# A paused generator is stopped only at the end of a weight tile

## The chip, the core and the metric

One NeuronCore of a Trainium2 chip runs the whole program. The metric is the device time of one execution in microseconds; shown is the median of several runs. TensorE (PE) multiplies matrices into PSUM, VectorE (DVE), ScalarE (ACT) and GpSimd (POOL) work element by element, SyncE (SP) issues the DMAs. The engines run side by side and wait for each other through semaphores; each works through its own instructions in a fixed order.

## The reference

The reference is a two-layer trunk for 1024 tokens of width 1024, in float32: a layer of RWKV-7 time mixing with an MLP, then a layer of forgetting attention with an MLP. What bears on the change is the dense work around the two mixers:

```python
y = y * ln_w.astype(jnp.float32) + ln_b.astype(jnp.float32)
...
y = (y + bonus.reshape(bsz, T, D_MODEL)).astype(h.dtype)
return (y * g) @ wo, v_first
...
x = x + (1.0 + gt1) * y
h = modulate(rms_norm(x, norm_mlp_g[i]), sh2, sc2)
x = x + (1.0 + gt2) * sq_relu_mlp(h, mlp_up[i], mlp_down[i])
...
def sq_relu_mlp(h, w_up, w_down):
    return jnp.square(jax.nn.relu(h @ w_up)) @ w_down
```

The width of the MLP is 4096. In `wo`, `w_up` and `w_down` lie most of the matrix products.

## The kernel before

Activations stand transposed, width on the 128 partitions, and the 1024 tokens are two halves of 512 columns. A float32 product is made of three products of a shorter float type: an operand `a` is split into a rounded part and the rest (`hh`, `hl` for activations of the projections, `mh`, `ml` inside the MLP, `wh`, `wl` for weights), and `mm3` (lines 120 to 128) issues rounded by rounded (L124), rounded weight by rest (L126) and rest of the weight by rounded (L128).

A weight tile is 128 x 1024 floats. `load_w` (L107) brings it into `wraw` by a DMA on SP's queue, casts it to `wh` on ACT (L116) and takes the difference `wl` on POOL (L117). Each of the three names has two buffers (`NW = (2, 2)`), shared by all streams of weights of the program. A buffer can be taken for a new tile when the last reader of the old tile is done. For one half of the tokens a weight tile serves 24 products of 512 columns.

`proj` (L150) multiplies one set of activations by a list of weight tiles; the first `lead` of them are loaded together. It is a generator that yields after each `mm3`, so that one stream of dense work can be advanced step by step beside something else. `mlp` is one too: sixteen chunks, each with two up tiles (`up`, through `proj`, 16 steps for one half) and two down tiles of the chunk before (`down`, 16 steps). A down tile holds four output blocks of two steps each; after the two steps DVE adds the block to the residual stream `x` (L1016). `take(g, n)` advances a generator by `n` steps, `drain` to its end, `beside` advances one at a given pace while another runs.

The first half's dense work of layer 0, called `m0`, runs beside the recurrent scan, which leaves PE time. When the scan ends, `run` (L347 ff.) goes on in this program order: activations of the second half are loaded and split (`gated(1, hp1)`), `m0` is taken `ND[0]` = 20 steps further, the second half's output projection (`wo`, eight tiles, `lead=2`) is run to its end, two steps of the second half's MLP `m1` make its norm (squares on ACT, L222; sums on POOL, L226; a product with a matrix of ones on PE, L228), `m0` is taken 40 steps and drained, and `m1` follows, beside the vectors of the next layer. In the last stage `phase_out` does the same with another `m0` of layer 1: it runs beside the second half's attention, is then taken `NF` = 36 steps, and the second half's output projection of attention follows.

The program order is only the first word: a scheduler that models the engines' time (`schedule_with_timeline_sim`) puts the instructions of each engine into their final order, and the buffers follow from the program order. In the names of the order, a number after a tile's name is the allocation, `pj`, `pk` are PSUM banks of products, `x06` is block 6 of the first half's residual stream, `x10` block 0 of the second half's; in attention `ps` are scores, `P0`, `P1` softmax tiles (exponentials on ACT, L1296), `pt` their transposes, `po` the sums of values.

Of the kernel before, what the change touches and what calls it, by code (L numbers as in the profile page):

```python
# [26 lines left out]
KT = 8  # L27
# [48 lines left out]
class K:  # L76
# [69 lines left out]
    def take(self, g, n):  # L146
        for _ in range(n):
            next(g, None)

    def proj(self, hs, src, mts, evac, lead=1):  # L150

        mts = list(mts)
        for g in [mts[:lead]] + [[m] for m in mts[lead:]]:
            w = [self.load_w(src(m)) for m in g]
            ps = [[self.bank() for _ in hs] for _ in g]
            for js in ([[j] for j in range(len(hs))] if len(g) > 1 else [range(len(hs))]):
                for k in range(KT):
                    for i in range(len(g)):
                        self.mm3([ps[i][j] for j in js], w[i][0][:, k], w[i][1][:, k], [hs[j] for j in js], k, k == 0, k == KT - 1)
                        yield  # L160
            for i, m in enumerate(g):
                for p, h in zip(ps[i], hs):
                    evac(m, h[0], p)
# [84 lines left out]
    def run(self, stop=99):  # L248
        tc, nc, ap = self.tc, self.nc, self.ap
        V, S = nc.vector, nc.scalar  # L250
        with ExitStack() as es:
# [49 lines left out]
            self.wp = self.pool(es, "wring", 3)  # L301
            self.weng = nc.gpsimd
            self.after_w = False
            pg = self.pool(es, "pg", space=PSUM)
            self.banks, self.nbank = [(pg, "pj", 2)], 0
            self.smalls, self.nsmall = [(pg, "pms", 1)], 0
# [15 lines left out]
            def beside():  # L322
                yield from dense
                el.close()
                self.xq = self.pool(e1, "x0", side="right")
                self.hp = self.pool(ed, "hp", 8, side="right")
                self.mid = self.pool(eg, "mid", 3, side="right")
                while self.ngated < KT:
                    yield
                x[0] = self.load_x(self.xq, 0)  # L330
                hs = self.gated(0, self.hp)
                yield from self.proj([hs], wo, range(KT), self.residual(x, self.G[:, 0:8]), lead=2)
                yield from self.mlp(x, 0, (0,), self.hp, self.mid)
            m0 = beside()
# [14 lines left out]
            with ExitStack() as e2:  # L349
                self.mod_pool = self.pool(e2, "mp"), 2, D  # L350
                hs = self.gated(1, hp1)
                self.take(m0, self.ND[0])
                self.drain(self.proj([hs], wo, range(KT), self.residual(x, self.G[:, 0:8]), lead=2))
                m1 = self.mlp(x, 0, (1,), hp1, md)
                self.take(m1, 2)
                self.take(m0, self.ND[1])
                self.drain(m0)
                self.take(m1, 40)

                def mods():  # L360
                    for j in range(6):
                        yield from self.layer_mod(1, j)
                    for j in range(2):
                        yield from self.mod(ap["kvmodw"], j * D, PC["kvmodb"] + j * 8, self.md[:, 96 + j * 8:104 + j * 8])
                self.after_w = True
                self.beside(mods(), m1, self.NMD)
                for o, j in ((16, 2), (24, 5)):
                    V.tensor_scalar(out=self.G[:, o:o + 8], in0=self.mdc(1, j), scalar1=1.0, scalar2=None, op0=ALU.add)
                self.gains(self.col("nmix1", 0, 8), self.mdc(1, 1), self.A[:, 16:24])
                self.gains(self.col("nmlp1", 0, 8), self.mdc(1, 4), self.A[:, 24:32])  # L370
                self.gains(self.col("kvg", 0, 8), self.md[:, 104:112], self.A[:, 32:40])
                self.take(m1, 100)
                rs = self.rs = [xq.tile([128, HT], F32, name=f"rs{j}") for j in range(2)]
                self.rms(x[0], rs[0])
                kv = self.norm_half(x, 0, rs[0], self.A[:, 32:40], self.md[:, 96:104], hp)
                q0 = self.norm_half(x, 0, rs[0], self.A[:, 16:24], self.mdc(1, 0), hp2)
                self.drain(m1)
# [652 lines left out]
    def mlp(self, x, l, js, hp, md):  # L1030

        nc, ap = self.nc, self.ap
        hs = []
        for j in js:
            rs = md.tile([128, HT], F32, name="mr", tag="mr", bufs=2)
            yield from self.rms_g(x[j], rs)
            hs.append(self.norm_half(x, j, rs, self.A[:, 8 + 16 * l:16 + 16 * l], self.mdc(l, 3), hp))
        gain = self.G[:, 8 + 16 * l:16 + 16 * l]
        mid = {}

        def up(c):
            def evac(m, j, ps):
                h = mid[m, j] = md.tile([128, HT], F32R, name="mh", tag="mh"), md.tile([128, HT], F32R, name="ml", tag="ml")
                r = md.tile([128, HT], F32, name="mr", tag="mr", bufs=2)
                nc.scalar.activation(out=r, in_=ps, func=AF.Relu)
                nc.vector.tensor_tensor(out=r, in0=ps, in1=r, op=ALU.mult)  # L1046
                self.split(*h, r)
            yield from self.proj(hs, lambda m: ap["up"][l][m], range(c * 2, c * 2 + 2), evac, lead=2 if c == 0 else 1)

        def down(c):  # L1050
            ms = [[(j, [mid[c * 2 + k, j][0] for k in range(2)], [mid[c * 2 + k, j][1] for k in range(2)]) for j in js]][0]
            evac = self.residual(x, gain)
            for q in range(2):
                wh, wl = self.load_w(ap["down"][l][c * 2 + q], (128, 2, 4, 128))
                for i in range(4):
                    ps = [self.bank() for _ in js]
                    for k in range(2):
                        self.mm3(ps, wh[:, k, i], wl[:, k, i], ms, k, k == 0, k == 1)
                        yield
                    for j, p in zip(js, ps):  # L1060
                        evac(q * 4 + i, j, p)

        yield from up(0)
        for c in range(1, 16):
            yield from up(c)
            yield from down(c - 1)
        yield from down(15)


# [138 lines left out]
    def phase_out(self, x, hp, pg, es):  # L1208
        with ExitStack() as em:
            md = self.pool(em, "mid1", 3, side="right")  # L1210

            def first():
                yield from self.out_fox(x, 0, hp)
                yield from self.mlp(x, 1, (0,), hp, md)
            m0 = first()
            with ExitStack() as ea:
                wp = self.pool(ea, "att1", 2)
                psa = self.pool(ea, "psa1", 1, space=PSUM)
                self.beside(self.attend(1, wp, psa), m0, self.NM)
            px = self.pool(es, "px2", space=PSUM)  # L1220
            self.banks = [(pg, "pj", 2)] * 2 + [(px, "pk", 4)] * 4
            self.smalls = [(pg, "pms", 1), (px, "pmt", 1)]
            hp1 = self.pool(es, "hp1", 8)
            md1 = self.pool(es, "mid2", 6)
            self.take(m0, self.NF)
            self.drain(self.out_fox(x, 1, hp1))
            m1 = self.mlp(x, 1, (1,), hp1, md1)
            self.take(m1, 2)
            self.drain(m0)
        self.take(m1, 100)  # L1230
        fin = self.pool(es, "fin", 8)
        self.beside(self.phase_final(x, 0, fin), m1, 4)
        self.drain(m1)
        self.drain(self.phase_final(x, 1, fin))
# [235 lines left out]
```

## Time and profile before

| | us |
|---|---|
| median of 3 runs (3393.43 to 3404.93) | 3394.25 |
| profiled execution | 3394.05 |
| its span, first to last instruction | 3392.1 |
| PE busy | 3214.4 |
| DVE busy | 1943.0 |
| ACT busy | 1432.8 |
| POOL busy | 1358.7 |

The profile shows one execution. Busy times of the engines overlap, so they don't add up to the span. A row of the view of stretches gives the busy time of each engine between two moments (counted from the start of the span) and the mean clock that TensorE was granted, as a share of full speed. A row of the view in time order gives the start of an instruction, its duration, its line and tiles, and in brackets how long its engine had been idle before it and which instruction released it. Products on PE are pipelined: their durations overlap, and the distance of two starts tells the pace.

### The profile page before, as it was taken

The page shows a single profiled execution, that of the slowest core. Times are in us where ns is not written, and L with a number is a line of the kernel's source. Part 1 is how long each engine was busy: PE and PEld are TensorE (multiplying, and loading weights), DVE is VectorE, ACT ScalarE, POOL GpSimd, SP SyncE. Part 2 cuts the span into 40 slices and gives each one's busy share as a digit, 9 for nine tenths or more (in the row PEclk, how much of TensorE's full clock was granted, in tenths as well). Part 3 has the DMA queues.
Part 4 walks back from the last instruction along what each step waited for, and adds up shares of the span by engine and source line. Part 5 has one row for each costly group of instructions (what it writes and reads, how often), then busy time and mean ns, then how long its engine had stood idle before and what let it go on. Part 6 is the DMA issues. An engine that isn't in the chain of part 4 may idle for free.

```text
span 3392.1 us, 50350 instructions
## 1 busy us (share of the span) xinstructions
PE 3214.4 (95%) x19108; PEld 2438.4 (72%) x19108; DVE 1943.0 (57%) x3239; ACT 1432.8 (42%) x2284; POOL 1358.7 (40%) x868
## 2 busy tenths in 40 slices
PE   4898999999999999899999999999999999999997
PEld 2456666666777776678887777777778888778886
DVE  7496765766556534167786433555566666454344
ACT  3642236523433223242233556667555544332323
POOL 3364432333333233354444432444423333454444
PEclk7899999899999999899999999999999999999999
DMA  7374344355333223236752233666544443232222
GB/s 276 98 234 151 95 128 135 116 152 150 88 102 102 85 76 125 68 111 224 229 187 88 85 131 119 207 203 182 177 128 136 144 134 100 88 111 95 98 98 83
DMA packets 294065, 452.90 MB, mean 134 GB/s; under 512 B 114720, under 2 KB 170432, under 8 KB 293824
## 3 DMA queue, kind: packets, MB, share of 16 engines
q1 hardware_dynamic: 293824, 449.68, 42.3%
q8 instruction: 152, 2.49, 0.3%
q14 instruction: 89, 0.73, 0.1%
HBM read 371.25 MB, written 78.32 MB: 133 GB/s over the span
## 4 chain that ended last, share of the span: by engine, by line
PE 50%; DVE 4%; ACT 2%; DMA 1%; issue 1%; POOL 1%; SPq 0%; DVEq 0%; ACTq 0%; POOLq 0%
PE pj L124 8%; PE pj L128 7%; PE pj L126 7%; PE pk L128 7%; PE pk L124 7%; PE pk L126 7%; PE pt L1328 2%; PE po L1313 1%; PE po L1314 1%; PE ps L1285 1%; PE ps L1286 1%; DVE t L239 1%; DVE hl L241 1%; DVE x L1016 1%; DVE modacc L185 0%
## 5 line engine op out<-in xcount | busy, mean ns | idle before, releaser
L117 POOL TENSOR_TENSOR wl<-wraw,wh 128x1024 fp32r<-128x1024 f32 x385 | 947.7, 2462 | 1231.7 <-ACT wh L116 1162.6
L116 ACT CAST wh<-wraw 128x1024 fp32r<-128x1024 f32 x385 | 402.6, 1046 | 822.0 <-PE pk L126 359.2
L124 PE MATMUL pj<-hh,wh 128*128 128x512 f32 x1120 | 448.6, 408 | 7.4 <-DVE sq L1090 2.7
L128 PE MATMUL pj<-hh,wl 128*128 128x512 f32 x1120 | 445.1, 403 | 5.5 <-POOL wl L117 5.5
L126 PE MATMUL pj<-hl,wh 128*128 128x512 f32 x1120 | 443.2, 401 | 0.0
L1016 DVE SCALAR_TENSOR_TENSOR x<-pj,G,x 128x512 f32<-128x512 f32 x304 | 225.8, 747 | 164.3 <-PE pj L128 162.2
L128 PE MATMUL pk<-hh,wl 128*128 128x512 f32 x688 | 272.1, 402 | 8.6 <-POOL wl L117 8.6
L124 PE MATMUL pk<-hh,wh 128*128 128x512 f32 x688 | 270.2, 398 | 8.9 <-ACT wh L116 7.8
L126 PE MATMUL pk<-hl,wh 128*128 128x512 f32 x688 | 267.3, 395 | 0.0
L124 PEld LDWEIGHTS pj<-hh,wh 128*128 128x128 f32 x1120 | 210.9, 189 | 61.9 <-issue 4.5
L1016 DVE SCALAR_TENSOR_TENSOR x<-pk,G,x 128x512 f32<-128x512 f32 x240 | 176.2, 746 | 135.7 <-PE pk L128 135.2
L128 PEld LDWEIGHTS pj<-hh,wl 128*128 128x128 f32 x1120 | 210.6, 188 | 58.9 <-POOL wl L117 7.7
L126 PEld LDWEIGHTS pj<-hl,wh 128*128 128x128 f32 x1120 | 211.1, 189 | 48.1 <-issue 2.4
L124 PE MATMUL pj<-mh,wh 128*128 128x512 f32 x564 | 236.9, 421 | 6.0 <-DVE mr L1046 3.0
L126 PE MATMUL pj<-ml,wh 128*128 128x512 f32 x564 | 224.3, 398 | 0.0
L128 PE MATMUL pj<-mh,wl 128*128 128x512 f32 x564 | 219.4, 399 | 2.4 <-POOL wl L117 2.4
L124 PE MATMUL pk<-mh,wh 128*128 128x512 f32 x460 | 182.1, 398 | 8.9 <-DVE mr L1046 5.4
L166 ACT CAST mh<-mr 128x512 fp32r<-128x512 f32 x128 | 79.5, 621 | 250.6 <-PE pj L128 109.1
L126 PE MATMUL pk<-ml,wh 128*128 128x512 f32 x460 | 181.7, 395 | 0.0
L185 DVE SCALAR_TENSOR_TENSOR modacc<-modw,cact,modacc 128x1024 f32<-128x1024 f32 x98 | 155.1, 1583 | 31.0 <-DMA modw<-in_modw_dram 22.5
L128 PE MATMUL pk<-mh,wl 128*128 128x512 f32 x460 | 166.6, 397 | 0.0
L124 PEld LDWEIGHTS pk<-hh,wh 128*128 128x128 f32 x688 | 130.7, 190 | 42.8 <-ACT wh L116 11.6
(334 smaller groups left out, 6493.2 us busy)
## 6 DMA issues: line engine op xcount, KB each, us to landing
wraw<-in_up_dram SPq DMA_DIRECT2D x128, 512.0 KB
wraw<-in_down_dram SPq DMA_DIRECT2D x128, 512.0 KB
modw<-in_modw_dram SPq DMA_DIRECT2D x96, 512.0 KB
wraw<-in_wqg_dram SPq DMA_DIRECT2D x32, 512.0 KB
wraw<-in_wk_dram SPq DMA_DIRECT2D x24, 512.0 KB
wraw<-in_wv_dram SPq DMA_DIRECT2D x24, 512.0 KB
x<-in_xT_dram SPq DMA_DIRECT2D x32, 256.0 KB
wraw<-in_wr_dram SPq DMA_DIRECT2D x16, 512.0 KB
```

The costliest lines, as they stand in the source:

```text
L116: nc.scalar.copy(out=wh, in_=raw)
L117: self.weng.tensor_tensor(out=wl, in0=raw, in1=wh.bitcast(F32), op=ALU.subtract)
L124: mm(out=p, lhsT=wh, rhs=hh[k], start=first, stop=False)
L126: mm(out=p, lhsT=wh, rhs=hl[k], start=False, stop=False)
L128: mm(out=p, lhsT=wl, rhs=hh[k], start=False, stop=last)
L166: self.nc.scalar.copy(out=out_h, in_=src)
L185: nc.vector.scalar_tensor_tensor(out=acc, in0=w, scalar=ck, in1=acc, op0=ALU.mult, op1=ALU.add)
L239: nc.vector.scalar_tensor_tensor(out=t, in0=x[k], scalar=A[:, k:k + 1], in1=rs, op0=ALU.mult, op1=ALU.mult)
L241: nc.vector.scalar_tensor_tensor(out=hl[k], in0=t, scalar=sh[:, k:k + 1], in1=hh[k].bitcast(F32), op0=ALU.add, op1=ALU.subtract)
L1016: self.nc.vector.scalar_tensor_tensor(out=x[j][m], in0=ps, scalar=gain[:, m:m + 1], in1=x[j][m], op0=ALU.mult, op1=ALU.add)
L1285: PE.matmul(out=o[:, 0:r], lhsT=qs[:, q], rhs=kh[:, i * n:i * n + r], start=True, stop=False)
L1328: PE.transpose(out=pt[:, i * 256 + b * 128:i * 256 + (b + 1) * 128], in_=Ps[b][:, (k + i) * 128:(k + i + 1) * 128], identity=ident)
```

## The change

A flag `partial` is kept: true after a step if some weight tile that the stream has loaded has products still to come, false after the last product of all loaded tiles. A new function `take_tiles` takes the given number of steps and then goes on until the flag is false. It replaces `take` at the two places where the first half's stream is stopped before the second half's projection.

```diff
+    def take_tiles(self, g, n):
+
+        self.take(g, n)
+        while self.partial:
+            next(g, None)
...
                 for k in range(KT):
                     for i in range(len(g)):
                         self.mm3([ps[i][j] for j in js], w[i][0][:, k], w[i][1][:, k], [hs[j] for j in js], k, k == 0, k == KT - 1)
+                        self.partial = not (js[-1] == len(hs) - 1 and k == KT - 1 and i == len(g) - 1)
                         yield
...
             self.after_w = False
+            self.partial = False
...
                 hs = self.gated(1, hp1)
-                self.take(m0, self.ND[0])
+                self.take_tiles(m0, self.ND[0])
                 self.drain(self.proj([hs], wo, range(KT), self.residual(x, self.G[:, 0:8]), lead=2))
...
                     for k in range(2):
                         self.mm3(ps, wh[:, k, i], wl[:, k, i], ms, k, k == 0, k == 1)
+                        self.partial = i < 3 or k == 0
                         yield
...
             md1 = self.pool(es, "mid2", 6)
-            self.take(m0, self.NF)
+            self.take_tiles(m0, self.NF)
             self.drain(self.out_fox(x, 1, hp1))
```

At the first place 20 steps end in the middle of a down tile, behind its second block of four; the loop goes on for four steps. At the second place 36 steps end where the flag is false, and nothing is added. All later lines of the file have numbers that are higher by 6 to 9.

On DVE, at the end of the scan, the residual updates show the order in which blocks are finished. Before (L1016 is the update):

```order
L1016 SCALAR_TENSOR_TENSOR x04_7389<-pj_12541,G_88,x04_7389 128x512
L1016 SCALAR_TENSOR_TENSOR x05_7390<-pj_12549,G_88,x05_7390 128x512
L1016 SCALAR_TENSOR_TENSOR x10_12379<-pk_12568,G_88,x10_12379 128x512
L1016 SCALAR_TENSOR_TENSOR x11_12380<-pk_12569,G_88,x11_12380 128x512
L1016 SCALAR_TENSOR_TENSOR x12_12381<-pk_12626,G_88,x12_12381 128x512
L1016 SCALAR_TENSOR_TENSOR x13_12382<-pk_12658,G_88,x13_12382 128x512
L1016 SCALAR_TENSOR_TENSOR x14_12383<-pj_12690,G_88,x14_12383 128x512
L1016 SCALAR_TENSOR_TENSOR x15_12384<-pj_12722,G_88,x15_12384 128x512
L1016 SCALAR_TENSOR_TENSOR x16_12385<-pk_12754,G_88,x16_12385 128x512
L1016 SCALAR_TENSOR_TENSOR x06_7391<-pk_12839,G_88,x06_7391 128x512
L1016 SCALAR_TENSOR_TENSOR x07_7392<-pk_12847,G_88,x07_7392 128x512
```

And DVE at the same place in the changed kernel (L1024 is the update now):

```order
L1024 SCALAR_TENSOR_TENSOR x04_7389<-pj_12541,G_88,x04_7389 128x512
L1024 SCALAR_TENSOR_TENSOR x05_7390<-pj_12549,G_88,x05_7390 128x512
L1024 SCALAR_TENSOR_TENSOR x06_7391<-pk_12557,G_88,x06_7391 128x512
L1024 SCALAR_TENSOR_TENSOR x07_7392<-pk_12565,G_88,x07_7392 128x512
L174 TENSOR_TENSOR ml_12491<-mr_12492,mh_12490 128x512
L1024 SCALAR_TENSOR_TENSOR x10_12379<-pk_12584,G_88,x10_12379 128x512
L1024 SCALAR_TENSOR_TENSOR x11_12380<-pk_12585,G_88,x11_12380 128x512
L1024 SCALAR_TENSOR_TENSOR x12_12381<-pj_12642,G_88,x12_12381 128x512
```

Blocks 6 and 7 of the first half, the last two of the down tile, moved from behind the seventh projection tile to ahead of the first; PE's products stand in the same order, and from PE's row 4056 of 13010 the two orders are alike up to row 8700.

On ACT, at the same place, before (L116 casts a weight tile, L222 squares a block of the second half):

```order
L116 CAST wh_12557<-wraw_12556 128x1024
L116 CAST wh_12563<-wraw_12562 128x1024
L222 ACTIVATE t_12814<-x10_12379 128x512
L116 CAST wh_12621<-wraw_12620 128x1024
L222 ACTIVATE t_12816<-x11_12380 128x512
```

And on ACT in the changed kernel (L173 is the split's cast, L229 the square):

```order
L116 CAST wh_12573<-wraw_12572 128x1024
L173 CAST mh_12490<-mr_12492 128x512
L116 CAST wh_12579<-wraw_12578 128x1024
L116 CAST wh_12637<-wraw_12636 128x1024
L229 ACTIVATE t_12830<-x10_12379 128x512
```

The split of m0's last up block, `mh_12490`, stood behind the last projection cast and now stands behind the first; its buffer comes free with the last products of the down tile.

On PE between rows 8700 and 9221, in the second half's attention beside the first MLP tiles of layer 1's `m0`, the scheduler orders some pieces differently. Before (L1285, L1286, L1288 are scores, L1328 transposes):

```order
L124 MATMUL pj_21832<-hh_21778,wh_21821 128x512
L124 MATMUL pj_21833<-hh_21778,wh_21827 128x512
L126 MATMUL pj_21832<-hl_21786,wh_21821 128x512
L128 MATMUL pj_21832<-hh_21778,wl_21822 128x512
L126 MATMUL pj_21833<-hl_21786,wh_21827 128x512
L128 MATMUL pj_21833<-hh_21778,wl_21828 128x512
L124 MATMUL pj_21832<-hh_21779,wh_21821 128x512
L124 MATMUL pj_21833<-hh_21779,wh_21827 128x512
L1285 MATMUL ps_22018<-kh_21488,qs_21489 128x448
L1286 MATMUL ps_22018<-ka_21490,qa_21491 128x448
```

And on PE in the changed kernel (L1294, L1295 and L1297 are the scores, L1337 the transposes):

```order
L124 MATMUL pj_21832<-hh_21778,wh_21821 128x512
L124 MATMUL pj_21833<-hh_21778,wh_21827 128x512
L1294 MATMUL ps_22018<-kh_21488,qs_21489 128x448
L1295 MATMUL ps_22018<-ka_21490,qa_21491 128x448
L1337 MATMUL pt_22041<-cs_60,P1_21927 128x128
L1337 MATMUL pt_22041<-cs_60,P0_21882 128x128
```

The scores of the next block stood behind the last step but one of the tile pair and now stand ahead of it. From row 9221 on the two orders are alike again.

## Rows read from the trace of the kernel before

**Rows 1.** The page: span, and PE's busy time, share and instruction count.

```profile
span 3392.1 us, 50350 instructions
...
PE 3214.4 (95%) x19108; PEld 2438.4 (72%) x19108; DVE 1943.0 (57%) x3239; ACT 1432.8 (42%) x2284; POOL 1358.7 (40%) x868
```

**Rows 2.** Stretches: start:end, length, busy us (count) by engine, PE clock, DMA share, GB/s.

```profile
1336.00:1414.00 78.00, 61.87 (x211) 45.17 (x211) 8.96 (x14) 13.13 (x17) 26.64 (x14) 0.87 0.17 55
1346.00:1356.00 10.00, 7.65 (x24) 5.49 (x24) 0.75 (x1) 1.61 (x2) 2.12 (x1) 0.83 0.15 53
1414.00:1464.00 50.00, 50.00 (x215) 39.89 (x214) 18.85 (x25) 13.93 (x18) 23.41 (x10) 1.00 0.29 93
```

**Rows 3.** PE's waits, 1336 to 1414: waiter <- releaser: total us, times, longest.

```profile
PE pk L128 <- POOL wl L117: 7.0, 5, 1.7
PE pk L124 <- ACT wh L116: 4.8, 5, 1.0
PE pj L128 <- POOL wl L117: 3.4, 2, 1.7
PE pj L124 <- ACT wh L116: 0.9, 1, 0.9
```

**Rows 4.** PE in time order: start, us, instruction, idle before [us <- releaser].

```profile
1336.52 0.40 PE L124 MATMUL pk<-hh,wh 128*128 128x512 f32 x1
...
1337.65 0.39 PE L124 MATMUL pk<-hh,wh 128*128 128x512 f32 x1
...
1342.21 0.39 PE L128 MATMUL pk<-hh,wl 128*128 128x512 f32 x1
1343.55 0.50 PE L124 MATMUL pk<-hh,wh 128*128 128x512 f32 x1 [0.95 <-ACT wh L116]
...
1345.98 0.50 PE L128 MATMUL pk<-hh,wl 128*128 128x512 f32 x1 [1.70 <-POOL wl L117]
...
1383.60 1.02 PE L228 MATMUL pmt<-t,ones_d 128*128 128x512 f32 x2
...
1405.27 0.50 PE L124 MATMUL pk<-hh,wh 128*128 128x512 f32 x1 [0.95 <-ACT wh L116]
...
1405.84 0.40 PE L124 MATMUL pk<-mh,wh 128*128 128x512 f32 x1
...
1408.64 0.39 PE L128 MATMUL pk<-hh,wl 128*128 128x512 f32 x1
...
1413.65 0.40 PE L124 MATMUL pj<-hh,wh 128*128 128x512 f32 x1
```

**Rows 5.** ACT and POOL in time order around the projection.

```profile
1333.73 1.05 ACT L116 CAST wh<-wraw 128x1024 fp32r<-128x1024 f32 x1 [2.34 <-PE pk L126]
1342.45 1.04 ACT L116 CAST wh<-wraw 128x1024 fp32r<-128x1024 f32 x1 [7.67 <-PE pk L126]
...
1408.14 0.62 ACT L166 CAST mh<-mr 128x512 fp32r<-128x512 f32 x1 [2.36 <-PE pk L128]
...
1334.85 2.40 POOL L117 TENSOR_TENSOR wl<-wraw,wh 128x1024 fp32r<-128x1024 f32 x1 [1.99 <-ACT wh L116]
```

**Rows 6.** Two weight loads, from issue on SP to the cast that waited.

```profile
412.63 0.40 SPq L115 DMA_DIRECT2D wraw<-in_wr_dram  x1
418.10 1.05 ACT L116 CAST wh<-wraw 128x1024 fp32r<-128x1024 f32 x1 [0.77 <-DMA wraw<-in_wr_dram]
...
538.62 0.42 SPq L115 DMA_DIRECT2D wraw<-in_wk_dram  x1
542.66 1.05 ACT L116 CAST wh<-wraw 128x1024 fp32r<-128x1024 f32 x1 [1.69 <-DMA wraw<-in_wk_dram]
```

**Rows 7.** Two stretches of the second half's attention, and one wait of PE.

```profile
2440.00:2471.00 31.00, 26.26 (x148) 21.05 (x146) 20.12 (x38) 19.31 (x39) 13.37 (x11) 0.93 0.48 140
2471.00:2600.00 129.00, 128.32 (x678) 106.46 (x679) 83.95 (x156) 68.19 (x146) 42.54 (x31) 0.98 0.44 130
...
2464.86 0.42 PE L1285 MATMUL ps<-kh,qs 128*128 128x320 f32 x1 [2.23 <-ACT P L1296]
```

## The prediction

> **What bounds the kernel now.** The page comes first: TensorE (PE) is busy for 3214.4 of 3392.1 us, so about 178 us of the span are PE idle time, and any time won has to come from there or from the clock [rows 1]. The profiled execution took 3394.05 us, 1.95 us more than its span and 0.2 us below the median of the three runs, so the sum is made against 3394.05 and read against the median unchanged.
>
> The view by stretches comes next, for the place that the diff names: the second half's output projection. Between 1336 and 1414 us PE is busy for only 61.87 of 78 us and its mean granted clock is 0.87; right behind it, in 1414 to 1464, the first half's MLP runs 50.00 of 50 us at clock 1.00, with weight tiles of the same size and again 24 products for each [rows 2]. So the hole belongs to the stage, not to this kind of work. The list of PE's waits says who makes it: 7.0 + 4.8 + 3.4 + 0.9 = 16.1 us, all for the two steps that split a weight tile, the cast `wh` on ACT and the difference `wl` on POOL [rows 3].
>
> In time order a pattern repeats. The first projection tile runs freely: 20 products start within 1342.21 - 1337.65 = 4.56 us, 0.228 us each. Then PE waits 0.95 us for `wh`, issues two products, waits 1.70 us for `wl`, and so on for every tile; the second tile starts at 1343.55 and the eighth at 1405.27, six periods of (1405.27 - 1343.55) / 6 = 10.29 us where 24 x 0.228 = 5.47 us is the work [rows 4]. ACT shows why: the cast at 1342.45 stood idle for 7.67 us and was let go by PE's L126, the last reader of the `wh` of the tile just finished [rows 5]. With two free buffers it would wait for the tile before that one. One of the two is missing: it holds the down tile of m0, whose last 12 products come only at 1405.84 to 1408.64, inside the eighth projection tile [rows 4].
>
> Of the 10.29 us, 5.47 is work and 2.65 is the two waits. The other 2.17 comes with the clock: in 1346 to 1356 the grant is 0.83, which between the levels of 1.2 and 2.4 GHz means that 3.4 of 10 us ran at half, 1.7 us of them lost [rows 2]; the remaining 0.5 is the slower start after a wait.
>
> **The change part by part.** The second call, in the last stage, adds nothing: 36 steps end there where m0's flag is already false, so no step is moved. The first call moves four steps of m0 ahead of the projection: 12 products and two residual updates on VectorE (DVE). Their weights are loaded and split, their operands exist, and no DMA is moved with them (the 8 projection loads keep their place on SP's queue).
>
> The stretch from the first projection product (1336.52) to the first product of m0's next tile (1413.65) takes 77.1 us now [rows 4]. Afterwards it holds:
> the 12 moved products, 1408.64 - 1405.84 = 2.8 us;
> 192 projection products at 0.228 us, 43.8 us;
> one norm sum (L228), now hidden in a wait, at its shown 1.02 us.
> That is 47.6 us, a gain of 29.5 us. With the pace of the next stretch, 50 us for 215 records or 0.2326 each [rows 2], the 192 cost 44.7 us and the gain is 28.6. I take 0.228, because it was measured on the same operands.
>
> What must hide behind PE for this? Each tile needs a cast (1.05 us) and a difference (2.40 us), about 3.5 us [rows 5], and with both buffers it has one whole tile time, 5.47 us, for that. A raw tile's slot is free again when its difference is done; two loads that were really waited for took 542.66 - 538.62 = 4.0 and 418.10 - 412.63 = 5.5 us from issue to the cast [rows 6]. Load, cast and difference make 7.5 to 9.0 us in the 10.9 us of two tiles. The norm's squares (ACT) and sums (POOL) lie in the rest.
>
> The tightest place is the second tile. On ACT the split of `mh`, which waited until 1408.14 for the held products, now stands between the first and the second projection cast. It can go when the 12 products end, at about 1336.5 + 2.8 = 1339.3; 0.62 for it, 1.05 and 2.40 for cast and difference, and the tile is ready near 1343.5, while PE asks for it at 1339.3 + 5.5 = 1344.8. The cover is 1.3 us. If it failed, one pattern of 4.8 us (10.29 - 5.47) would be back. The first tile's cast and difference stay at 1333.73 and 1334.85 [rows 5] and are now covered by the moved products. For small waits left over I put 0.5 us, between 0 and 4.8, near the low end because the next stretch with the same two buffers shows none.
>
> From row 4056 of PE to row 8700 the order is what it was, so everything until about 2471 us should only come earlier. From there to row 9221 the scheduler orders attention of the second half and m0's first MLP tiles differently: scores come before instead of after the last steps of a tile pair. That stretch, 2471 to 2600, is 128.32 of 129 us busy [rows 7], so at most 0.7 us can be won. Loss is bounded by the 31 us before it, where one chain of waits (2.23 us for a softmax tile the longest) cost 31 - 26.26 = 4.7 us of idle time and a mean clock of 0.93, another 2.2 us [rows 7]; about 7 us for such a break. I take 0, by the stretch's own row.
>
> Sum: 3394.05 - 29.5 + 0.5 = 3365 us.
>
> **Rivals.**
> A, the helpers become the bound. Two buffers free, but loads or splits late, so that a tile takes longer than 5.47 us. It decides when a load needs over 10.9 - 3.5 = 7.4 us. A load of 9 us would make a tile (9 + 3.5) / 2 = 6.25 us, eight of them 6 us more: 3371 us. Against it: the loads of 4.0 and 5.5 us, and the next stretch without a wait.
>
> B, only the pauses come back. If the half clock had another cause than the pauses, the gain would be the 16.1 us of rows 3: 3378 us. For it: no single pause is longer than 1.70 us, yet the clock falls in every period. Against it: the clock is 1.00 in the stretch behind, with the same work and no pause. The Trainium skill, TensorE: Matmul & The Clock Gate, section What's actually happening, puts half clock down to an idle engine and full clock to a busy one; taken strictly, these short pauses with products between them leave the engine busy, the fall would be something else, and 3378 us would follow. The trace speaks against that reading, as said.
>
> C, the change doesn't do what it says: the missing buffer is held by something else and the pattern stays. The time would be 3394 us. Against it: the cast's releaser is the tile just finished, and the pattern ends with the held products.
>
> D, slower: breaks like the one before 2471 us in the reordered attention. About 40 places in the order of PE differ there; at 7 us for each break four would eat the gain, and beyond 0.5% slower it needs (29 + 17) / 7 = 7 of them: 3411 us and more. For it: the transposes of a softmax tile now come sooner behind its scores, with a weight cast and a ReLU ahead of the exponentials on ACT. Against it: those chains lie between long products, as in the 128.32 of 129 us now.
>
> **How the numbers follow.** Forecast 0.86, A 0.05, B 0.03, C 0.04, D 0.02. The forecast's own range goes from 3394.05 - 29.5 - 0.7 = 3364 to 3365 + 7 = 3372; the low end gets some 4 us more for the spread between executions, the high end 3 us for A and a second small wait: 3360 to 3375. About 0.5%, 17 us, is what a measurement of this kernel can tell from no change. Faster by more than that, below 3377: forecast and A, 0.91. Within it: B and C, 0.07. Slower: D, 0.02.
>
> **What would show it.** Right: in the stretch of the second half's projection some 48 us instead of 77, PE busy throughout at clock 1.00, no wait for `wh` or `wl`, and casts let go by the tile before the last; everything up to the attention of the second half 29 us earlier, and the loss of clock near 2450 unchanged. Wrong: PE waits on the raw loads or on `wl` of the second tile (A), a clock below 1 without pauses (B), the old period of 10.3 us (C), or new PE waits for softmax tiles behind about 2440 us (D). The forecast fails as a whole if the projection was already hidden behind something that ends later; but PE is the only engine that works on there, and what follows waits for its products.

## The result, and the profile after

| | before | after |
|---|---|---|
| median of the runs | 3396.16 us (4 runs, 3393.43 to 3404.93) | 3369.24 us (4 runs, 3365.42 to 3374.15) |
| profiled execution | 3394.05 us, span 3392.1 | 3365.42 us, span 3363.6 |
| stage of the second half's projection | 77.13 us | 47.26 us |

The medians differ by 26.9 us. The ratio that is estimated from the single executions is 0.9915, with a 95% interval of 0.9899 to 0.9931, which is 28.9 us faster, 23.4 to 34.3. The forecast was 3365, in a range of 3360 to 3375, and a gain of 29 us. In the profiled executions the times differ by 28.63 us.

The page of after, its span and engines, answers [rows 1]. PE is busy for 15.7 us less with the same 19108 instructions; the span lost 28.5 us, so 12.8 us of it are idle time that went and 15.7 are time in which the same instructions ran slower before.

```profile
span 3363.6 us, 50344 instructions
...
PE 3198.7 (95%) x19108; PEld 2433.9 (72%) x19108; DVE 1952.5 (58%) x3239; ACT 1433.0 (43%) x2284; POOL 1360.2 (40%) x868
```

The stretches of after that answer [rows 2] (start:end, length, busy time and count by engine, granted PE clock, DMA share, GB/s): the projection, then m0's next MLP tiles.

```profile
1336.00:1384.00 48.00, 48.00 (x211) 39.25 (x210) 9.87 (x14) 12.79 (x16) 27.75 (x14) 1.00 0.29 93
1385.00:1435.00 50.00, 50.00 (x214) 39.94 (x213) 18.93 (x25) 14.03 (x18) 23.38 (x10) 1.00 0.26 89
```

The 211 PE records that took 78 us before fill 48 us now, without a gap and at clock 1.00, the level of 2.4 GHz. The list of PE's waits, which had 16.1 us for `wh` and `wl` in [rows 3], is empty between 1300 and 1440 us. PE in time order shows what stands there instead of [rows 4]:

```profile
1337.48 0.39 PE L124 MATMUL pk<-mh,wh 128*128 128x512 f32 x1
...
1340.05 0.40 PE L128 MATMUL pk<-mh,wl 128*128 128x512 f32 x1
1340.28 0.40 PE L124 MATMUL pk<-hh,wh 128*128 128x512 f32 x1
...
1384.74 0.40 PE L124 MATMUL pj<-hh,wh 128*128 128x512 f32 x1
```

The 12 held products (`mh`) run first, from 1337.48; the projection (`hh`) starts at 1340.28, and m0's next tile at 1384.74. That is 1384.74 - 1337.48 = 47.26 us where it was 1413.65 - 1336.52 = 77.13. ACT and POOL of after, for the second projection tile and the next two, against [rows 5]:

```profile
1339.78 0.62 ACT L173 CAST mh<-mr 128x512 fp32r<-128x512 f32 x1 [4.04 <-PE pk L128]
1340.31 1.05 ACT L116 CAST wh<-wraw 128x1024 fp32r<-128x1024 f32 x1
1345.78 1.05 ACT L116 CAST wh<-wraw 128x1024 fp32r<-128x1024 f32 x1 [4.42 <-PE pk L126]
...
1351.22 1.05 ACT L116 CAST wh<-wraw 128x1024 fp32r<-128x1024 f32 x1 [3.84 <-PE pk L126]
...
1341.44 2.65 POOL L117 TENSOR_TENSOR wl<-wraw,wh 128x1024 fp32r<-128x1024 f32 x1 [3.21 <-ACT wh L116]
```

The releaser still reads L126, but the times say which tile it belongs to. Before, a cast was let go and PE stood waiting for that same cast. Now the cast at 1345.78 starts when the first projection tile ends (1340.28 + 5.47 = about 1345.75) and makes the third tile, which PE asks for one tile time later; the second tile has been split since 1341.44 + 2.65 = 1344.09. The weights are one tile ahead again. In the built programs the placement of `wh` in SBUF says the same: before, all eight projection tiles lie at one address and the down tile of m0 at the other; after, the eight alternate between the two.

Last, the attention that the scheduler ordered anew. The list of PE's waits between 2400 and 2600 us, four rows of PE in time order, and the two stretches of [rows 7], 26.4 us earlier:

```profile
PE ps L1294 <- ACT P L1305: 2.4, 2, 2.2
PE pj L124 <- ACT hh L247: 1.1, 1, 1.1
PE po L1322 <- DVE r L1352: 0.8, 1, 0.8
PE pt L1337 <- DVE tl L174: 0.5, 1, 0.5
```

```profile
2438.49 0.41 PE L1294 MATMUL ps<-kh,qs 128*128 128x320 f32 x1 [2.23 <-ACT P L1305]
...
2444.61 1.22 PE L124 MATMUL pj<-hh,wh 128*128 128x512 f32 x2 [1.08 <-ACT hh L247]
...
2463.48 0.50 PE L1294 MATMUL ps<-kh,qs 128*128 128x512 f32 x1 [0.21 <-ACT P L1305]
...
2574.96 0.36 PE L1294 MATMUL ps<-kh,qs 128*128 128x448 f32 x1
```

```profile
2413.60:2444.60 31.00, 26.27 (x147) 20.93 (x145) 20.09 (x38) 19.29 (x39) 13.39 (x11) 0.94 0.47 140
2444.60:2573.60 129.00, 128.77 (x688) 107.40 (x689) 87.25 (x156) 69.65 (x148) 43.05 (x32) 0.99 0.45 130
```

The old wait of 2.23 us for a softmax tile stands where it stood, 2464.86 - 2438.49 = 26.4 us earlier, and the stretch around it has the busy time and the clock that it had (26.27 and 0.94; 26.26 and 0.93 before). Behind it there is one new wait for a softmax tile, of 0.21 us at 2463.48. The stretch of 129 us is as full as before (128.77, and 128.32 before). The score product at 2574.96 is this one in before:

```profile
2603.20 0.36 PE L1285 MATMUL ps<-kh,qs 128*128 128x448 f32 x1
```

From the old wait to it PE takes 2574.96 - 2438.49 = 136.47 us in after and 2603.20 - 2464.86 = 138.34 in before.

### The profile page after: what moved, and what is told of

The parts are those of the page before. It is cut to its first block, busy times and chain, and to the rows that moved or that the text cites. A ratio compares the mean times of both kernels' runs of the same rounds, so it can differ in the third digit from the quotient of the medians.

```text
span 3363.6 us, 50344 instructions
## 1 busy us (share of the span) xinstructions
PE 3198.7 (95%) x19108; PEld 2433.9 (72%) x19108; DVE 1952.5 (58%) x3239; ACT 1433.0 (43%) x2284; POOL 1360.2 (40%) x868
## 5 line engine op out<-in xcount | busy, mean ns | idle before, releaser
L116 ACT CAST wh<-wraw 128x1024 fp32r<-128x1024 f32 x385 | 402.7, 1046 | 798.3 <-PE pk L126 332.8
L126 PE MATMUL pj<-hl,wh 128*128 128x512 f32 x1120 | 440.4, 399 | 0.0
L1024 DVE SCALAR_TENSOR_TENSOR x<-pj,G,x 128x512 f32<-128x512 f32 x304 | 225.8, 747 | 155.3 <-PE pj L128 152.2
L126 PE MATMUL pk<-hl,wh 128*128 128x512 f32 x688 | 265.7, 393 | 0.0
L1024 DVE SCALAR_TENSOR_TENSOR x<-pk,G,x 128x512 f32<-128x512 f32 x240 | 176.3, 746 | 117.4 <-PE pk L128 111.3
L126 PEld LDWEIGHTS pj<-hl,wh 128*128 128x128 f32 x1120 | 209.4, 187 | 47.1 <-issue 2.4
L126 PE MATMUL pj<-ml,wh 128*128 128x512 f32 x564 | 224.5, 398 | 0.0
L173 ACT CAST mh<-mr 128x512 fp32r<-128x512 f32 x128 | 79.5, 621 | 251.7 <-PE pj L128 111.0
L126 PE MATMUL pk<-ml,wh 128*128 128x512 f32 x460 | 181.7, 395 | 0.0
L126 PE MATMUL pj<-xl,wh 128*128 128x512 f32 x320 | 138.0, 432 | 21.3 <-DVE xl L174 21.3
```

Of the source, the lines that this page charges most:

```text
L116: nc.scalar.copy(out=wh, in_=raw)
L126: mm(out=p, lhsT=wh, rhs=hl[k], start=False, stop=False)
L173: self.nc.scalar.copy(out=out_h, in_=src)
L1024: self.nc.vector.scalar_tensor_tensor(out=x[j][m], in0=ps, scalar=gain[:, m:m + 1], in1=x[j][m], op0=ALU.mult, op1=ALU.add)
```

## The experiments

The theory: two buffers serve every split weight tile, one is held by the unfinished down tile of m0, so the projection has a ring of one. Against it stood that the work moved ahead matters, that the half clock has a cause of its own, and that the effect is peculiar to this place. Two numbers of the kernel set where m0 is stopped: `ND[0]`, the steps before the layer-0 projection, and `NF`, those before the layer-1 projection. Five of the seven kernels are the kernel before with such numbers changed, one is the kernel before with two lines added, and one is the changed kernel again; the runs of the kernel before that each is compared with were made beside it on the same chip.

**Half of the moved work, buffer still held.**

```diff
-    ND = (20, 40)
+    ND = (22, 38)
```

> The kernel before, but the first half's stream is stopped two steps later (22 instead of 20): half of the moved work (6 products, one block) comes ahead of the projection, while the down tile still has two steps to come. If the held weight buffer makes the hole, nothing of it goes: periods of about 10.3 us per projection tile, PE waits of some 15 to 16 us for wh and wl, about 3394 us. If the moved work itself is what helps, because it covers the splits of the first tiles, half of the gain shows: about 3380 us.

Measured: 3398.42 us (median of 10 runs), ratio 0.9999 (0.9989 to 1.0009). PE's waits between 1325 and 1425 us, and the stretch of [rows 2], in this kernel:

```profile
PE pk L128 <- POOL wl L117: 7.2, 5, 1.7
PE pk L124 <- ACT wh L116: 3.8, 4, 1.0
PE pj L128 <- POOL wl L117: 3.4, 2, 1.7
PE pj L124 <- ACT wh L116: 1.9, 2, 1.0
```

```profile
1336.00:1414.00 78.00, 61.64 (x210) 44.94 (x209) 8.70 (x11) 14.39 (x18) 26.70 (x14) 0.87 0.19 61
```

7.2 + 3.8 + 3.4 + 1.9 = 16.3 us of waits, as before (16.1), and the same hole. Two of the four steps ahead of the projection bring nothing as long as the tile is not finished.

**One step short of the tile's end.** The scheduler then takes the last step ahead of the projection by itself.

```diff
-    ND = (20, 40)
+    ND = (23, 37)
```

> The kernel before, stopped after 23 steps, one short of the tile's end. The scheduler itself puts the last step ahead of the projection here, so that both buffers are free in time although the stop lies inside the tile. If free buffers are what counts, this is as fast as the changed kernel: a stage of some 47 us, no waits for wh and wl, 3365 to 3370 us. If the place of the stop in the program counts, it stays near 3394 us.

Measured: 3371.12 us (4 runs), ratio 0.9918 (0.9902 to 0.9935). PE has no wait between 1325 and 1425 us, and the stretch of 48 us is full; the row ahead of it is the last product of the held tile:

```profile
1342.20 0.39 PE L128 MATMUL pk<-mh,wl 128*128 128x512 f32 x1
```

```profile
1336.00:1384.00 48.00, 48.00 (x211) 39.20 (x210) 11.59 (x17) 13.84 (x17) 26.01 (x13) 1.00 0.30 99
```

So the stop as written is not what counts. The last product of the held tile runs at 1342.20, just inside the first projection tile, which starts at 1341.74. What counts is whether it stands ahead of the second projection tile on PE; in the placement of this program the two buffers alternate, as in after.

**The end of the tile before: less work ahead, no buffer held.**

```diff
-    ND = (20, 40)
+    ND = (16, 44)
```

> The kernel before, stopped after 16 steps, at the end of the down tile ahead: no tile is held, and four steps less than before lie ahead of the projection instead of four more. If the held buffer is the cause, the projection runs at 5.5 us a tile again and the time is 3365 to 3372 us, the upper end if the first tile is not ready when PE comes to it some 5.6 us earlier than in the changed kernel. If it is the extra work ahead that helps, the time is 3394 us or more.

Measured: 3366.73 us (4 runs, 3360.69 to 3374.03), ratio 0.9909 (0.9890 to 0.9928), and the stretch of 48 us of this kernel:

```profile
1336.00:1384.00 48.00, 48.00 (x211) 39.25 (x210) 8.59 (x13) 13.05 (x17) 28.44 (x15) 1.00 0.28 92
```

Four steps fewer ahead than before, eight fewer than after, and the same gain within the intervals. Together with the first run this takes the moved work out of the explanation: any stop at a tile's end frees the buffer.

**Shorter pauses, buffer still held.** The difference `wl` of the projection is made on DVE instead of POOL; the ring of one stays.

```diff
                 self.take(m0, self.ND[0])
+                self.weng = nc.vector
                 self.drain(self.proj([hs], wo, range(KT), self.residual(x, self.G[:, 0:8]), lead=2))
+                self.weng = nc.gpsimd
```

> The kernel before with the difference wl of the eight projection tiles taken on DVE instead of POOL; the buffer is still held. A difference of 128x512 takes 0.69 to 0.84 us on DVE, so one of 128x1024 about 1.5 us against 2.40, and the wait for wl shrinks from 1.70 to about 0.8 us, that for wh stays at 0.95. If the half clock comes with pauses of any length, it stays: period about 9.4 us, some 6 us won, 3388 us. If the shorter pauses leave the clock up, period about 7.3 us, some 21 us won, 3373 us.

Measured: 3382.3 us (4 runs), ratio 0.9952 (0.9937 to 0.9967): 16.3 us less by the ratio, 14.1 between the medians. PE in time order in this kernel, with the idle time ahead of an instruction and its releaser; the first and last row the start and the end of the stage; then PE's waits between 1325 and 1425 us, 4.5 + 2.7 + 1.1 + 0.9 = 9.2 us; one difference on DVE; and the stretch:

```profile
1338.92 0.40 PE L124 MATMUL pk<-hh,wh 128*128 128x512 f32 x1
...
1346.32 0.50 PE L124 MATMUL pk<-hh,wh 128*128 128x512 f32 x1 [0.91 <-ACT wh L116]
...
1347.58 0.50 PE L128 MATMUL pk<-hh,wl 128*128 128x512 f32 x1 [0.53 <-DVE wl L117]
...
1353.79 0.50 PE L124 MATMUL pk<-hh,wh 128*128 128x512 f32 x1 [0.91 <-ACT wh L116]
...
1399.51 0.40 PE L124 MATMUL pj<-hh,wh 128*128 128x512 f32 x1
```

```profile
PE pk L124 <- ACT wh L116: 4.5, 5, 0.9
PE pk L128 <- DVE wl L117: 2.7, 5, 0.6
PE pj L128 <- DVE wl L117: 1.1, 2, 0.5
PE pj L124 <- ACT wh L116: 0.9, 1, 0.9
```

```profile
1346.30 1.23 DVE L117 TENSOR_TENSOR wl<-wraw,wh 128x1024 fp32r<-128x1024 f32 x1
```

```profile
1336.00:1384.00 48.00, 40.18 (x162) 28.98 (x160) 16.41 (x20) 10.72 (x13) 5.04 (x3) 1.00 0.23 77
```

The difference takes 1.23 us on DVE (2.40 on POOL), the wait for it falls from 1.70 to 0.53 us, and the period from 10.29 to 1353.79 - 1346.32 = 7.47 us. Only 0.95 + 1.70 - 0.91 - 0.53 = 1.21 of these 2.82 us are shorter waits. The slower start after a wait is still there: 7.47 - 5.47 - 0.91 - 0.53 = 0.56 us, where the prediction had put 0.5. So the rest, 1.6 us, is the clock, which is 1.00 throughout although PE still pauses for every tile. Six periods of 2.82 us less are 16.9 us; the stage shrank from 77.13 to 1399.51 - 1338.92 = 60.6, by 16.5 us. The half clock of the kernel before went when only the pauses got shorter, so here it came with them. Which of the two pauses brings it, and how long one has to be, these runs don't tell. The other 13 us, to the 47.26 of after, are the ring of one itself: the 9.2 us of waits and some 0.56 us of slower start for each of seven tiles.

**The same hole at the other projection.** In layer 1 the kernel before stops m0 at a tile's end (36 steps). Here the stop in layer 0 is at a tile's end, 24, and the one in layer 1 is moved into a tile.

```diff
-    ND = (20, 40)
+    ND = (24, 36)
...
-    NF = 36
+    NF = 34
```

> The changed kernel's first stop (24 steps) and, at the second place in the last stage, a stop after 34 steps instead of 36: there the stream now stops two steps short of a weight tile's end, and the eight tiles of the second half's attention projection (lead 1) all get the same buffer, where 36 gives them two in turn. If the held buffer is the cause wherever it is held, the pattern of the first place appears at the second: seven changes of tile at about 4.8 us (10.29 - 5.47), some 29 to 33 us, so about the time of the kernel before, 3395 to 3402 us. If the first place was special (the end of the scan, loads of x and y beside it), it stays at 3365 to 3374 us.

Measured: 3399.85 us (10 runs) beside 3398.77 of the kernel before (17 runs), ratio 0.9995 (0.9984 to 1.0006): the gain of layer 0 is there (the first stretch below) and layer 1 has taken all of it back. PE in time order around the layer-1 projection of this kernel, and two stretches:

```profile
2863.47 0.50 PE L124 MATMUL pj<-hh,wh 128*128 128x512 f32 x1 [0.95 <-ACT wh L116]
...
2865.90 0.79 PE L128 MATMUL pj<-hh,wl 128*128 128x512 f32 x1 [1.70 <-POOL wl L117]
...
2873.55 0.50 PE L124 MATMUL pj<-hh,wh 128*128 128x512 f32 x1 [0.95 <-ACT wh L116]
```

```profile
1336.00:1384.00 48.00, 48.00 (x209) 39.04 (x208) 15.87 (x21) 16.05 (x21) 25.40 (x13) 1.00 0.33 112
2860.00:2880.00 20.00, 14.69 (x49) 10.64 (x48) 1.50 (x2) 3.20 (x4) 5.94 (x3) 0.83 0.17 52
```

The same two pauses to the hundredth, a first period of 2873.55 - 2863.47 = 10.08 us, the clock at 0.83 again: the pattern belongs to the held buffer and not to layer 0.

**The hole in a smaller dose.** As above with `NF` = 32; in the placement of this program only the first five of the eight projection tiles lie at one address.

```diff
-    ND = (20, 40)
+    ND = (24, 36)
...
-    NF = 36
+    NF = 32
```

> As the run before, with a stop after 32 steps: the scheduler puts the held steps ahead of the sixth projection tile here, and only the first five of the eight tiles share one buffer. If each change of tile on one buffer costs the same, four of them make 4 x 4.8 = 19 us over the changed kernel, about 3386 to 3390 us. If the hole depends only on whether a tile is held at the stop, it is as slow as with 34 steps.

Measured: 3384.51 us (6 runs), ratio 0.9952 (0.9931 to 0.9973), 16.2 us over the median of the changed kernel on the same chip. PE in time order at the tile changes of this kernel, and the first two periods as stretches:

```profile
2854.32 0.50 PE L124 MATMUL pk<-hh,wh 128*128 128x512 f32 x1 [0.95 <-ACT wh L116]
...
2856.75 0.50 PE L128 MATMUL pk<-hh,wl 128*128 128x512 f32 x1 [1.70 <-POOL wl L117]
...
2862.99 0.50 PE L124 MATMUL pj<-hh,wh 128*128 128x512 f32 x1 [0.95 <-ACT wh L116]
...
2865.42 0.80 PE L128 MATMUL pj<-hh,wl 128*128 128x512 f32 x1 [1.70 <-POOL wl L117]
...
2873.14 0.50 PE L124 MATMUL pj<-hh,wh 128*128 128x512 f32 x1 [0.95 <-ACT wh L116]
...
2875.62 0.50 PE L128 MATMUL pj<-hh,wl 128*128 128x512 f32 x1 [0.34 <-POOL wl L117]
```

```profile
2854.30:2863.00 8.70, 6.03 (x25) 4.37 (x25) 0.75 (x1) 1.63 (x3) 2.36 (x1) 1.00 0.18 60
2863.00:2873.10 10.10, 7.49 (x24) 5.42 (x24) 0.75 (x1) 1.54 (x3) 3.59 (x2) 0.83 0.17 52
```

By the medians four tile changes within the shared buffer instead of seven cost about half, 16.2 of the 31.6 us that lie between 3399.85 and 3368.27 (below), but the runs scatter from 3375.80 to 3396.78. The forecast of this run, 4 x 4.8 = 19 us, took every change to cost the same, and the trace, of the execution of 3375.80, shows that they don't. Only the first two have both pauses at full length. At the third the held products of m0 run while POOL makes the difference, and 0.34 us of that pause are left; the fourth has 0.57 and 0.23 us. From the last product of attention to the second norm sum behind it this execution takes 11.7 us longer than the profiled one of the changed kernel (89.4 and 77.7 us); with `NF` = 34 it is 29.5 longer (107.2).

The first two changes also part the pauses from the clock. They have the same two pauses, but the first period takes 2862.99 - 2854.32 = 8.67 us at clock 1.00 and the second 2873.14 - 2862.99 = 10.15 us at 0.83. So such a pair of pauses does not bring the half clock every time, and where it does the clock costs 10.15 - 8.67 = 1.5 us.

**The changed kernel beside the two.**

> The changed kernel once more, beside the kernel before on the same chip, for a closer ratio: the stage gave 29.9 us, so a ratio of about 0.9913, and the two levels of time that its first four executions showed (3365 and 3373 us) should be seen again in both kernels if they do not belong to the change.

Measured: 3368.27 us (5 runs, 3364.21 to 3373.62), ratio 0.9901 (0.9882 to 0.9920), which holds the 0.9913 that was expected. The two levels of time, 3365 and 3373 us, did not come again: the five executions took 3364.21, 3368.02, 3368.27, 3368.34 and 3373.62 us. The stretch in layer 1 where the two runs above have their holes:

```profile
2860.00:2880.00 20.00, 20.00 (x90) 16.57 (x89) 2.65 (x4) 5.86 (x8) 12.75 (x7) 1.00 0.26 82
```

Not tried: a third buffer for `wh` and `wl`, which would leave the stop where it was and still free a buffer. It doesn't fit in SBUF beside the other tiles.

## Why the prediction was right, step by step

**The hole is a ring of one.** Held in every test. The buffer freed without the stop as written (23), and with less work ahead (16), gave the gain; more work ahead with the buffer held (22) gave nothing; the hole could be made again elsewhere (34), and in a smaller size (32). That rules out rival C and any gain from the moved products as such.

**The sum of the stage.** 47.6 us were forecast, 47.26 came, a gain of 29.9 instead of 29.5. The 12 products took 1340.28 - 1337.48 = 2.80 us, as put. The projection and the norm sum took 1384.74 - 1340.28 = 44.46 us, where 43.8 + 1.02 = 44.8 were put.

**The second tile.** The cover was put at 1.3 us: ready near 1343.5, asked for at 1344.8. It was ready at 1344.09 and asked for about 1345.75, 1.7 us later. The order of events was as forecast (split of `mh`, cast, difference), except that the split could go at 1339.78, before the last of the held products. The 0.5 us for small waits were not needed. That the sum met the profiled execution within half a microsecond is luck in part: 0.4 us more in this stage, 1.0 us lost ahead of it and the differences behind it (below) almost cancel.

**Rival B, the half clock.** The prediction took the half clock to come with the pauses, mainly because the next stretch has no pause and no loss. That was an argument from another stretch; the run with shorter pauses is the direct one, since only the engine of one operation was changed in the stage. The size was put right too: 1.7 us of clock loss in a period were reckoned from the 0.83, and 1.5 (in the run with `NF` = 32) and 1.6 (against the run on DVE) were measured. The Trainium skill, TensorE: Matmul & The Clock Gate, has two sections that bear on it. What's actually happening, taken strictly as the prediction did, would have left the clock low; A second HAM failure mode: psum-queue depth-cycling tells of a kernel whose many small idle times between groups of products made the clock swing between its levels. This case goes with the second: 0.83 of the clock with 0.95 and 1.70 us in each 10.29 us, 1.00 with 0.91 and 0.53 us in each 7.47 us. It does so only in part, as the one period of 8.67 us at 1.00 shows.

**Rival A, the helpers.** POOL and ACT keep up: ACT still idles for 3.84 us ahead of a cast and never has PE waiting.

**The rest of the program.** The claim that everything behind the stage only comes earlier holds within some 3 us, not exactly. At 1249.87 us of before and 1250.94 of after (the same product behind a residual update, in a part that the change does not touch) the profiled executions are already 1.1 us apart; 0.96 of that is left at the stage's start, and so 28.9 of the 29.9 us arrive at its end. At the score product near 2440 us 26.4 are left. Part of the difference is in a query projection, where PE's waits for a weight tile are these in after

```profile
2119.11 0.51 PE L124 MATMUL pj<-hh,wh 128*128 128x512 f32 x1 [0.69 <-ACT wh L116]
...
2121.62 0.50 PE L128 MATMUL pj<-hh,wl 128*128 128x512 f32 x1 [1.77 <-POOL wl L117]
```

and only this in before.

```profile
2148.25 0.50 PE L128 MATMUL pj<-hh,wl 128*128 128x512 f32 x1 [1.26 <-POOL wl L117]
```

0.69 + 1.77 - 1.26 = 1.2 us. The chain of waits of after passes there through the tile's load (5.65 us from 2113.57) and its difference (2.35 us from 2119.22). Why the load ends later against PE than before was not tried. At the score product of 2574.96 the difference is 2603.20 - 2574.96 = 28.2 us again, and at the end of the span 28.5.

**The reordered attention (rival D).** Put at 0, between -0.7 and +7. PE's waits between 2400 and 2600 us sum up to 2.4 + 1.1 + 0.8 + 0.5 = 4.8 us in after; the stretch of 129 us has 0.2 us of idle time (0.7 before). No break came; the sign for D, new waits for softmax tiles, showed once, with 0.21 us. The bound of 0.7 us on what could be won counted idle time alone: from the old wait to the same score product 138.34 - 136.47 = 1.9 us are gone. The new order is not shown to have won them. Three of the profiled executions have the old order in this stretch (before, the stop at 22 and the difference on DVE) and take 138.34, 135.86 and 138.17 us; the six with the new order take 135.46 to 136.82. So the order lost nothing, and what it may have won is not clear of the scatter.

**The size of the median.** The forecast was made against one execution and met the one profiled, 3365.42 against 3365. The median of after is 4 us higher, because its four executions differ: 3365.42 and 3365.51 with a mean granted clock of 0.973, 3372.97 and 3374.15 with 0.969. The kernel before scatters as far, 3393.43 to 3404.93. The prediction allowed some 4 us below for this and nothing above. Its 10 us above were put there for other things, 7 for a break in the reordered attention and 3 for rival A and a second small wait; that they held the highest execution too, by 0.85 us, is luck. Where in the span the clock is lost in the higher executions was not looked for.

## What to carry to other kernels

A stream that is paused in the middle of a tile keeps the tile's buffer, and in a ring of two it leaves the next stage a ring of one: every load and split then stands between two tiles, here 4.8 us for each tile whose products take 5.47. The trace shows it by a cast that is let go by the last reader of the tile just finished while the engine behind it waits for that very cast; stop such a stream at a tile's end, the earlier one will do as well as the next. Cost the pauses with the clock that they take along, and give the range above the forecast as much room for the scatter of executions as the range below.

## What the runs showed of the hardware

The granted clock did not follow the mere presence of pauses. With 0.95 + 1.70 us of them in 10.29 us PE got 0.83; with 0.91 + 0.53 us in 7.47 us it got 1.00, in all of the stage. Both the length of the pauses and their distance changed between these two, so neither is shown to be what decides. With `NF` = 32 the same 0.95 + 1.70 us left the clock at 1.00 in one period, of 8.67 us, and came with 0.83 in the next, of 10.15 us. Of the 16.5 us that the stage won by moving one operation to another engine, 16.1 - 9.2 = 6.9 are shorter waits, and the larger part, 9.6, goes with the clock.

The difference of two f32 tiles of 128x1024 took 1.23 us on DVE and 2.40 us on POOL.
